# Small products of the scan and the attention in longer runs, both weight parts of the time steps in one operand, row sums of the modulation put off: a two-layer diffusion block on one core

## The chip, the core and the metric

The program runs on one core of one Trainium2 chip. The metric is the device time of one execution in microseconds (us), lower is better; the time before is the median of three runs. TensorE is PE in the profile, VectorE DVE, ScalarE ACT, GpSimd POOL; SP starts the transfers.

## The reference

Two layers over 256 context and 256 latent tokens of width 1024, everything in float32. Cut to what the change touches:

```
for layer in range(2):
    mod_l = split(silu(c) @ ada_w[layer] + ada_b[layer], 6)       # modulation, latent
    mod_c = split(silu(c_ctx) @ ada_w[layer] + ada_b[layer], 6)   # modulation, context
    h = modulate(rms_norm(tokens), shift, scale)
    # three branches on the same h, each gated, summed, projected
    #  scan (16 heads x 64, 2 groups, state 128, chunks of 128, forward and backward):
    dt = softplus(h @ w_dt + dt_bias); cs = cumsum(dt * a) in a chunk
    scores = einsum('bclgn,bcsgn->bcgls', cm, bm)
    y_diag = einsum('bcgls,bcgels,bcsgep->bclgep', scores, exp(cs_l - cs_s), x * dt)
    states = einsum('bcsgn,bcsge,bcsgep->bcgepn', bm, exp(cs_end - cs), x * dt)
    y_off  = einsum('bclgn,bcgepn,bclge->bclgep', cm, h_in, exp(cs))
    #  attention (8 heads x 64): context queries see 256 context keys; latent queries see
    #  a window of the latent grid plus all context keys (512 keys with a bias and mask)
    p = softmax(q @ k.T * 64 ** -0.5 + bias); o = p @ v
    #  conformer: gated linear unit, depthwise convolution of 31, layer norm, silu
    tokens += gate * (merged @ w_o)
    # then a gated feed-forward: dense in layer 0, top 2 of 8 experts in layer 1
```

Layer 1 computes latent tokens alone behind its keys, values and scan states.

## The kernel before

**Main products.** Every weight product runs as three products of two reduced-precision parts ("hi" and "lo", type fp32r): hi*hi, hi*lo, lo*hi. `wstat` (lines 205 to 207) keeps the weight as the stationary operand and streams 512 or 256 tokens; `wmov` (lines 251 to 253) streams the weight. `split` (lines 116 and 117) makes the parts: ACT copies to hi, DVE subtracts to lo. Small products (scores, transposes, scan) run in plain float32, two passes each but for the transposes.

**Order.** Each layer goes through a list of steps; for layer 0 `glu dt qkv xbc ssd g1 p1 g2 p2 z g0 p0`, where `xbc`, `z` and `g`/`p` (gate and branch projection) are main products and `ssd`, and behind qkv the attention, start generators. After each group of main products `pump` lets every running generator go on by its rate. A generator yields a number, its price in those units. So attention, scan, conformer and modulation are strewn between main products, and the compiler's scheduler fixes the order of each engine from priorities.

**Late issue.** `behind()` orders what is issued in it after the last main product on PE. `defer(queue, f, depth=2)` puts a piece of work in a queue and issues the oldest one so, once more than `depth` wait. `undefer` empties the queue.

**Banks and buffers.** Small results share four PSUM banks (`pw`), main sums have the other four (`acc`). A `pw` bank comes free when its reader (an ACT or DVE instruction) has read it; the next small product that gets it waits for that on PE, and the main products behind it wait too.

**Attention** (`attention`; scores L750 for latent, L770 for context queries). A head pair has heads j = 0, 1, whose 64-wide products lie in the two halves of the array's rows (64\*128 in the profile). Latent: for each of two query blocks, scores of both heads, bias add and maxima on DVE (L754 to L757), exp on ACT (L758, L759), then per head and block one deferred piece that transposes P on PE (L740) and copies it out (L742), and last `values` (L786, 128\*64: the array's columns halved). Scaling of P is L733.

**Scan** (`ssd`; the y part ends in L1094). For a chunk, a group of 8 heads and a direction r, in two halves of 4 heads (`hq`): M = exp of decays by ACT (L1054, L1055), times scores by DVE (L1056), and deferred the product of M with x\*dt (tile ydS, L1063, 128\*64, 4 heads). Then for each direction with a carried state E = exp(cs) (L1077), yoS (L1080) and adds on DVE. States: stS (L954), one per direction.

**Time steps** (`dt_path`, L865 to L867): 32 columns, eight blocks of k, three products each.

**Modulation** (`ada_v`): DVE accumulates weight rows times silu(c) (tile adac, L374) as the weights arrive over two buffers; a 32-column product (L382, 128\*32) sums over the partitions, for two column blocks j and the streams s; DVE adds it to the bias (L385). It runs as a generator, for layer 0 during z, g0 and p0, for layer 1 during the dense feed-forward.

Of the kernel before, what the change touches and what calls it, by code (L numbers as in the profile page):

```python
# [53 lines left out]
class Body:  # L54
# [298 lines left out]
    def ada_v(self, l, g):  # L353
# [6 lines left out]
        for j0 in (0, 2):  # L360
            accs = []
            for j in (j0, j0 + 1):
# [3 lines left out]
                for k in range(KD):  # L366
# [8 lines left out]
                    yield 0.7 * len(streams)  # L375
                    if j == 1 and k == 0:
                        self.keep()

            ps = self.pw(f"ada{l}{g}{j0}")
            for s in streams:  # L380
                for j, acc in zip((j0, j0 + 1), accs):
                    nc.tensor.matmul(ps[32 * j:32 * j + 32], self.con("oc")[:, 1 - s:33 - s], acc[:, s * 512:(s + 1) * 512],  # L382
                                     start=(s == streams[0]), stop=(s == 1), skip_group_check=True)
# [333 lines left out]
    def attention(self, l, q, kT, v, nt, o_):  # L717
# [4 lines left out]
        q_ = []  # L722
        for q0, nk, lat in streams:
            nkb = nk // 128
            for hp in range(4):
# [5 lines left out]
                def turn(P, j, qb, PT=PT, nm=nm, nk=nk, nkb=nkb, st=st):  # L731

                    nc.vector.tensor_scalar(P, P, st[:, j, qb, 5:6], None, op0=ALU.mult)  # L733

                    def turned():
                        if not PT:
                            PT.update({i: self.t4(f"PT{nm}{i}").rearrange("p (k t) -> p k t", t=256) for i in range(2)})
                        pt = self.pw(f"PT{nm}{j}{qb}")
                        for kb in range(nkb):
                            nc.tensor.transpose(pt[:, kb * 128:(kb + 1) * 128], P[:, kb * 128:(kb + 1) * 128], self.con("id"))  # L740
                        ev = nc.scalar.copy if j else nc.vector.tensor_copy
                        ev(PT[j][:, :nkb, qb * 128:(qb + 1) * 128], pt[:, :nk].rearrange("p (k t) -> p k t", t=128))  # L742
                    self.defer(q_, turned)
                if lat:
                    for qb in range(2):
# [17 lines left out]
                        for j in range(2):  # L763
                            turn(P[j], j, qb)
                            yield 1.7
                else:
# [6 lines left out]
                    for j in range(2):  # L773
# [5 lines left out]
                        for qb in range(2):  # L779
                            turn(P[j][:, qb * 256:(qb + 1) * 256], j, qb)  # L780
                        yield 1.5
# [7 lines left out]
                self.defer(q_, values)  # L789
                yield 0.5  # L790
        yield from self.undefer(q_)

# [61 lines left out]
    def dt_path(self, l):  # L854
# [3 lines left out]
        wH = self.t2("wdtH" + nm, F32R)[:, :KD * 32].rearrange("p (k n) -> p k n", k=KD)  # L858
        wL = self.t2("wdtL" + nm, F32R)[:, :KD * 32].rearrange("p (k n) -> p k n", k=KD)
        with self.prio("w"):  # L860
            nc.sync.dma_start(w, self.a["w_dt"][l])
            self.split(w, wH, wL)
# [6 lines left out]
        nc.scalar.activation(dT[0:32, :], ps[0:32, :], AF.Copy)  # L869
        pt = self.pw("dtt" + nm)  # L870
        for b in range(NB):
            nc.tensor.transpose(pt[:, b * 32:(b + 1) * 32], dT[0:32, b * 128:(b + 1) * 128], self.con("id")[0:32, 0:32])
# [5 lines left out]
        nc.vector.tensor_tensor(b3(x), b3(pt[:, :n]), bc(self.col("dtb")), op=ALU.add)  # L878
# [50 lines left out]
    def ssd(self, l, nt):  # L929
# [9 lines left out]
        def states(b, dirs, use):  # L939
# [6 lines left out]
            for g in range(G):  # L946
                px = self.xs_t(b, g, "s" + nm)
                for r in dirs:
                    xe = self.t2(f"xe{nm}{b}{r}{g}")
                    nc.vector.tensor_tensor(hd(xe), hd(px), hb(we, b, r, g), op=ALU.mult)  # L950

                    def state(r=r, g=g, xe=xe):
                        ps = self.pw(f"st{nm}{b}{r}{g}")
                        nc.tensor.matmul(ps, Bp[:, g * 128:(g + 1) * 128], xe, start=True, stop=True)  # L954
                        use(r, g, ps)
                    self.defer(q_, state)
                    yield 1.8
# [58 lines left out]
    def ssd_y(self, nm, b, hin, q_):  # L1016
# [23 lines left out]
        for g in range(G):  # L1040
# [5 lines left out]
            st = {}  # L1046
            for r in range(2):
                load(*((1, g) if r == 0 else (0, g + 1)))
                pb = cb[r, g]
                for hq in range(2):  # L1050
                    h0 = g * 8 + hq * 4
                    M = self.t2(f"M{nm}{b}{g}{r}{hq}").rearrange("p (h l) -> p h l", h=4)
                    for i in range(4):
                        nc.scalar.activation(M[:, i, :], pb[:, hq * 4 + i, :], AF.Relu, bias=cs[:, b, r, h0 + i:h0 + i + 1], scale=-1.0)  # L1054
                    nc.scalar.activation(M, M, AF.Exp, scale=-1.0)  # L1055
                    nc.vector.tensor_tensor(M, M, scm[:, r, g, None, :].to_broadcast([128, 4, 128]), op=ALU.mult)  # L1056

                    def diag(r=r, hq=hq, M=M, g=g, xd=xd, st=st):
                        if "pd" not in st:
                            st["pd"] = self.pw(f"yd{nm}{b}{g}")  # L1060
                        for i in range(4):
                            hl = hq * 4 + i
                            nc.tensor.matmul(st["pd"][64 * (i % 2):64 * (i % 2) + 64, (hl // 2) * 128:(hl // 2 + 1) * 128],  # L1063
                                             xd[r][:, hl * 64:(hl + 1) * 64], M[:, i, :],
# [747 lines left out]
```

## Time and profile before

| quantity | value |
|---|---|
| median of 3 runs | 2364.38 us (2364.26 to 2365.93) |
| the profiled execution | 2367.87 us |
| its span in the profile | 2366.1 us |
| TensorE's mean granted clock | 0.978 |
| PE busy | 2226.4 us, 94% of the span |
| DVE busy | 1509.5 us, 64% |
| ACT busy | 1030.1 us, 44% |
| the chain that ended last | PE 71%, issue 11%, DVE 7%, DMA 6%, ACT 4% |

Durations below come from the profiled execution, 3.5 us longer than the median. The end of a matmul is modelled, and matmuls overlap: a row's duration is longer than the time to the next start, so the costs here are taken from start to start. The program's stages in the profile: modulation and norms to 55 us, mixer of layer 0 to some 690, dense feed-forward to 1090, mixer of layer 1 to 1545, experts to the end.

### The profile page before, as it was taken

To read this page: it belongs to the slowest core of one execution; us is meant where nothing else is said; L and a number is where in the kernel's file an instruction comes from. 1 tells how busy PE (TensorE), PEld (TensorE's weight loads), DVE (VectorE), ACT (ScalarE), POOL (GpSimd) and SP (SyncE) were. 2 spreads that over 40 slices of the span, in tenths; PEclk is the share of its full clock that TensorE was granted. 3 is DMA by queue.
4 is the path that set the end of the run, shared out by engine and by line. 5 is a ranking of instruction groups with operands and counts; after the bars stand their busy time and mean duration, and the time that the engine had idled before them with its cause. 6 is when DMAs were issued, how large, how long until landed. Compare 5 with 4: busy or idle time off the path is not lost.

```text
span 2366.1 us, 29723 instructions
## 1 busy us (share of the span) xinstructions
PE 2226.4 (94%) x11075; PEld 1632.5 (69%) x11075; DVE 1509.5 (64%) x2384; ACT 1030.1 (44%) x1658; POOL 17.4 (1%) x32
## 2 busy tenths in 40 slices
PE   7999999699999999999999889899999989999897
PEld 3776677477777777788877779766655656566564
DVE  3667999787667665536898765743433555565556
ACT  4334673643342222225347685443332345454453
POOL 0000000000000000000000000000000000000000
PEclk9999999899999999999999999999999999999998
DMA  7232253445445556423423344488888899999995
GB/s 269 95 117 72 76 172 127 116 156 169 147 143 160 173 175 199 147 98 102 147 89 104 107 146 161 139 324 330 341 320 320 330 365 375 357 385 347 348 370 206
DMA packets 123658, 492.51 MB, mean 208 GB/s; under 512 B 12784, under 2 KB 23792, under 8 KB 89712
## 3 DMA queue, kind: packets, MB, share of 16 engines
q1 hardware_dynamic: 122656, 487.89, 57.4%
q10 hardware_dynamic: 848, 2.62, 0.3%
q8 instruction: 89, 1.46, 0.2%
q14 instruction: 65, 0.53, 0.1%
HBM read 488.24 MB, written 2.23 MB: 207 GB/s over the span
## 4 chain that ended last, share of the span: by engine, by line
PE 71%; issue 11%; DVE 7%; DMA 6%; ACT 4%; POOL 0%; SPq 0%; POOLq 0%; DVEq 0%; ACTq 0%
PE er L1546 8%; PE nn L1428 7%; PE e L1546 4%; DMA adaw<-in_ada_w_dram 4%; PE ndn L1453 4%; PE edr L1546 3%; PE ed L1546 2%; PE wg L205 2%; PE wg L207 2%; PE wg L206 2%; DVE adac L374 2%; PE xbcL L205 1%; PE xbcL L206 1%; PE xbcL L207 1%; PE fu L206 1%
## 5 line engine op out<-in xcount | busy, mean ns | idle before, releaser
L374 DVE SCALAR_TENSOR_TENSOR adac<-adaw,sc,adac 128x512 f32<-128x512 f32 x224 | 160.1, 747 | 57.3 <-DMA adaw<-in_ada_w_dram 56.7
L117 DVE TENSOR_TENSOR l_er<-r_er,h_er 128x1024 fp32r<-128x1024 f32 x132 | 154.5, 1218 | 59.9 <-ACT h_er L116 59.5
L1428 PE MATMUL nn<-r_ngun,xn 128*64 128x512 f32 (+1 forms) x768 | 168.2, 561 | 0.0
L116 ACT ACTIVATE h_er<-r_er 128x1024 fp32r<-128x1024 f32 x132 | 133.0, 1053 | 42.2 <-DMA r_er<-in_moe_gu_dram 29.4
L205 PE MATMUL wg<-hHm,h_wg 128*128 128x512 f32 (+1 forms) x384 | 135.7, 355 | 1.8 <-ACT g L682 1.1
L206 PE MATMUL wg<-hLm,h_wg 128*128 128x512 f32 (+1 forms) x384 | 129.9, 339 | 0.0
L207 PE MATMUL wg<-hHm,l_wg 128*128 128x512 f32 (+1 forms) x384 | 128.8, 339 | 0.5 <-DVE l_wg L117 0.4
L1546 PE MATMUL er<-h_er,gHp 128*128 128x512 f32 (+1 forms) x288 | 110.5, 389 | 17.7 <-ACT h_er L116 17.7
L1428 PEld LDWEIGHTS nn<-r_ngun,xn 128*64 128x64 f32 x768 | 54.2, 137 | 91.9 <-issue 85.1
L1546 PE MATMUL er<-h_er,gLp 128*128 128x512 f32 (+1 forms) x288 | 108.1, 381 | 0.0
L117 DVE TENSOR_TENSOR l_e<-r_e,h_e 128x1024 fp32r<-128x1024 f32 x44 | 52.2, 1222 | 63.5 <-ACT h_e L116 62.6
L1453 PE MATMUL ndn<-r_ndn,hnn 128*64 128x512 f32 x352 | 87.4, 598 | 0.0
L572 DVE SCALAR_TENSOR_TENSOR ccv<-cu,cols,ccv 128x488 f32<-128x488 f32 (+14 forms) x120 | 84.5, 729 | 1.0
L1443 DVE TENSOR_TENSOR hnn<-npn,nsn 128x256 f32<-128x256 f32 (+1 forms) x24 | 9.6, 401 | 117.6 <-ACT nsn L1441 117.6
L1433 ACT ACTIVATE ntn<-nn 128x512 f32<-128x512 f32 (+1 forms) x24 | 13.5, 561 | 162.7 <-PE nn L1428 162.7
L1546 PE MATMUL er<-l_er,gHp 128*128 128x512 f32 (+1 forms) x288 | 84.3, 381 | 0.0
L205 PEld LDWEIGHTS wg<-hHm,h_wg 128*128 128x128 f32 x384 | 72.7, 189 | 14.5 <-issue 4.0
L1546 PEld LDWEIGHTS er<-h_er,gHp 128*128 128x128 f32 x288 | 54.8, 190 | 40.2 <-ACT h_er L116 29.0
L116 ACT ACTIVATE h_wg<-r_wg 128x1024 fp32r<-128x1024 f32 x48 | 50.6, 1058 | 71.8 <-PE wg L206 52.0
L117 DVE TENSOR_TENSOR l_edr<-r_edr,h_edr 128x1024 fp32r<-128x1024 f32 x66 | 77.0, 1217 | 4.4 <-ACT h_edr L116 4.1
L207 PEld LDWEIGHTS wg<-hHm,l_wg 128*128 128x128 f32 x384 | 72.2, 189 | 10.1 <-DVE l_wg L117 2.1
L206 PEld LDWEIGHTS wg<-hLm,h_wg 128*128 128x128 f32 x384 | 72.8, 190 | 8.8 <-issue 2.3
(642 smaller groups left out, 5955.5 us busy)
## 6 DMA issues: line engine op xcount, KB each, us to landing
r_ngun<-in_moe_gu_dram SPq DMA_DIRECT2D x88, 1024.0 KB, 7.1
r_er<-in_moe_gu_dram SPq DMA_DIRECT2D x66, 1024.0 KB, 7.3
r_ndn<-in_moe_down_dram SPq DMA_DIRECT2D x44, 1024.0 KB, 7.6
adaw<-in_ada_w_dram SPq DMA_DIRECT2D x160, 256.0 KB, 3.1
r_edr<-in_moe_down_dram SPq DMA_DIRECT2D x33, 1024.0 KB, 7.4
r_wg<-in_w_in_dram SPq DMA_DIRECT2D x48, 512.0 KB, 3.6
r_e<-in_moe_gu_dram SPq DMA_DIRECT2D x22, 1024.0 KB, 7.6
cbS<-csd SPq DMA_DIRECT2D x24, 512.0 KB, 4.9
```

Source lines behind the costliest of these rows:

```text
L116: nc.scalar.activation(Hd, src, AF.Copy)
L117: nc.vector.tensor_tensor(Ld, src, Hd.bitcast(F32), op=ALU.subtract)
L205: mm(out, wh, xh, start=(first and kk == 0), stop=False, skip_group_check=True)
L206: mm(out, wh, xl, start=False, stop=False, skip_group_check=True)
L207: self.last = mm(out, wl, xh, start=False, stop=(kk == kc - 1), skip_group_check=True).ins
L374: nc.vector.scalar_tensor_tensor(d, w, c, d, op0=ALU.mult, op1=ALU.add)
L572: nc.vector.scalar_tensor_tensor(y[:, :, a:b], x[:, :, a + s:b + s], w[:, k:k + 1], y[:, :, a:b], op0=ALU.mult, op1=ALU.add)
L1428: mm(ps[64 * h:64 * h + 64, :n], x[kk], w[:, h, k, :], start=(kk == 0), stop=(kk == KD - 1), skip_group_check=True)
L1433: nc.scalar.activation(t, ps[:, :n], AF.Copy)
L1443: nc.vector.tensor_tensor(d, v[:, :, 1], g, op=ALU.mult)
L1453: mm(ps[64 * h:64 * h + 64], hT[:, kk * 64:(kk + 1) * 64], w[:, h, k, :], start=(kk == 0), stop=(kk == fc - 1), skip_group_check=True)
L1546: mm(ps[s][j], st[kk], w[p][:, k, :], start=(kk == 0 and p == 0 and q == 0), stop=(kk == kc - 1 and p == 1), skip_group_check=True)
```

## The change

- Row sums of the modulation (`ada_v`): one more yield before them, and all of a group issued in one `behind()`; the accumulation steps yield 0.64 for 0.7.
- Attention: a piece of transposes now covers both heads (and, for context queries, both query blocks; the copy out is twice as wide and half as many); depth 1 for 2. `values` is put in a list `joined` and issued by the next piece of transposes, ahead of them. Scores of a latent query block come with the price 3.4 in one yield.
- Time steps: hi and lo parts lie side by side as 64 columns, streamed once with the tokens' hi part; the tokens' lo part meets the 32 hi columns. The two halves of the sum are added on DVE behind the transposes.
- Scan: the products of both halves `hq` and of the directions' yoS in one deferred piece per direction; states of both directions in one piece; depth 1; E's loads are issued with the last M. The order of the adds changes, not their number.

```
-            ps = self.pw(f"ada{l}{g}{j0}")
-            for s in streams:
-                for j, acc in zip((j0, j0 + 1), accs):
-                    nc.tensor.matmul(ps[32 * j:32 * j + 32], ...
+            yield len(streams)
+            ps = self.pw(f"ada{l}{g}{j0}")
+            with self.behind():
+                for s in streams:
+                    for j, acc in zip((j0, j0 + 1), accs):
+                        nc.tensor.matmul(ps[32 * j:32 * j + 32], ...
...
+                    def turned():
...
+                        pts = [self.pw(f"PT{nm}{j}{qbs[0]}") for j in range(2)]
+                        n = len(qbs) * 128
+                        for f in joined:
+                            f()
+                        joined.clear()
+                        for j in range(2):
+                            for kb in range(nkb):
+                                for i, qb in enumerate(qbs):
+                                    c = kb * n + i * 128
+                                    nc.tensor.transpose(pts[j][:, c:c + 128], P[j][qb][:, kb * 128:(kb + 1) * 128], self.con("id"))
...
+                    self.defer(q_, turned, 1)
...
-                        for j in range(2):
-                            turn(P[j], j, qb)
-                            yield 1.7
+                        turn([{qb: p} for p in P], (qb,))
+                        yield 3.4
...
-                self.defer(q_, values)
-                yield 0.5
+                self.defer(q_, lambda f=values: joined.append(f), 1)
...
         for k in range(KD):
-            nc.tensor.matmul(ps[0:32, :], wH[:, k, :], self.h[0][k], start=(k == 0), stop=False)
-            nc.tensor.matmul(ps[0:32, :], wH[:, k, :], self.h[1][k], start=False, stop=False)
-            nc.tensor.matmul(ps[0:32, :], wL[:, k, :], self.h[0][k], start=False, stop=(k == KD - 1))
+            nc.tensor.matmul(ps[0:64, :], wp[:, k, :], self.h[0][k], start=(k == 0), stop=False, skip_group_check=True)
+            nc.tensor.matmul(ps[0:32, :], wp[:, k, 0:32], self.h[1][k], start=False, stop=(k == KD - 1), skip_group_check=True)
...
+                def diag(r=r, M=M, g=g, xd=xd, st=st, E=E):
...
+                    for hl in range(8):
+                        nc.tensor.matmul(st["pd"][...], xd[r][:, hl * 64:(hl + 1) * 64], M[r, hl // 4][:, hl % 4, :], ...
...
+                self.defer(q_, diag, 1)
+                yield 1.8 if r == 0 else 4.2
```

**PE in `xbc` of layer 0, scores of latent queries.** xbcL is the main product, PT are transposes, S scores (two in a row are heads 0 and 1 of one query block), po the values of an earlier head pair; what an instruction waits for stands behind it. Before:

```order
L750 MATMUL S_1641<-kTL_0_702,qL_0_700 128x512 [waits Activation_49]
L740 MATMUL PT_1632<-con_t,P_1566 128x128
L750 MATMUL S_1642<-kTL_0_702,qL_0_700 128x512 [waits PE_49]
L740 MATMUL PT_1632<-con_t,P_1566 128x128
L740 MATMUL PT_1662<-con_t,P_1567 128x128 [waits Activation_49]
...
L205 MATMUL xbcL_3_1518<-hHm_257,h_xbcL_3_1746 128x512
L206 MATMUL xbcL_3_1518<-hLm_259,h_xbcL_3_1746 128x512
L786 MATMUL po_1689<-PT_1583,vL_0_704 64x256 [waits DVE_49]
```

In the changed kernel:

```order
L751 MATMUL PT_1588<-con_t,P_1522 128x128 [waits DVE_49,PE_49,Activation_49]
...
L762 MATMUL S_1602<-kTL_0_694,qL_0_692 128x512
L762 MATMUL S_1603<-kTL_0_694,qL_0_692 128x512
L762 MATMUL S_1660<-kTL_0_694,qL_0_692 128x512 [waits Activation_49]
L762 MATMUL S_1661<-kTL_0_694,qL_0_692 128x512 [waits DVE_49]
L207 MATMUL xbcL_3_1495<-hHm_257,l_xbcL_3_1730 128x512
L797 MATMUL po_1686<-PT_1539,vL_0_696 64x256 [waits Activation_49]
```

The scores of two query blocks now stand together (four heads in a run, no transposes between), and the values, which need a fifth `pw` bank, come one main product behind them and wait for an ACT reader.

**PE in `g1` of layer 0, the scan's products.** wg is the main product, ydS the product of M with x\*dt, xtyS transposes, yoS the carried state's part. Before:

```order
L206 MATMUL wg_3_2433<-hLm_258,h_wg_0_2436 128x512
L1063 MATMUL ydS_2482<-MS_2419,xdS_2413 64x128 x4
L926 MATMUL xtyS_2569<-con_t,uL_4_1139 128x128 x2
...
L207 MATMUL wg_0_2430<-hHm_256,l_wg_1_2497 128x512
L1063 MATMUL ydS_2482<-MS_2454,xdS_2413 64x128 x4
L205 MATMUL wg_1_2431<-hHm_256,h_wg_1_2496 128x512
```

In the changed kernel:

```order
L207 MATMUL wg_0_2402<-hHm_256,l_wg_1_2468 128x512
L1094 MATMUL ydS_2488<-MS_2395,xdS_2389 64x128 x4
L1094 MATMUL ydS_2488<-MS_2426,xdS_2389 64x128 x4
L942 MATMUL xtyS_2537<-con_t,uL_4_1131 128x128 x2
L942 MATMUL xtyS_2537<-con_t,uL_6_1132 128x128 x2
L205 MATMUL wg_1_2403<-hHm_256,h_wg_1_2467 128x512
```

Two runs of four heads with ten main products between them have become one run of eight.

**PE in the dense feed-forward, row sums of the modulation.** fg, fu and fd are the main products, ada the row sums. Before:

```order
L207 MATMUL fg_2_5939<-hHf_5370,l_fg_2_6016 128x512
L382 MATMUL ada_6447<-adac_6031,con_t 32x512
L205 MATMUL fg_3_5940<-hHf_5370,h_fg_2_6015 128x512
...
L382 MATMUL ada_6447<-adac_6238,con_t 32x512
L382 MATMUL ada_6447<-adac_6031,con_t 32x512
L205 MATMUL fu_3_6103<-hHf_5370,h_fu_2_6182 128x512
...
L382 MATMUL ada_6447<-adac_6238,con_t 32x512
```

In the changed kernel:

```order
L253 MATMUL fd_1_6402<-h_fd_0_6407,f0L_0_5486 128x512
L384 MATMUL ada_6423<-adac_6007,con_t 32x512
L384 MATMUL ada_6423<-adac_6190,con_t 32x512
L384 MATMUL ada_6423<-adac_6007,con_t 32x512
L384 MATMUL ada_6423<-adac_6190,con_t 32x512
L251 MATMUL fd_2_6403<-h_fd_0_6407,f0H_0_5485 128x512
```

The four sums of a group, strewn over three places some 100 main products apart, stand in one run, some 100 main products later than the last of them stood.

## Rows read from the trace of the kernel before

**Rows 1.** Page, part 1: busy us (share of the span) and instructions of each engine

```profile
PE 2226.4 (94%) x11075; PEld 1632.5 (69%) x11075; DVE 1509.5 (64%) x2384; ACT 1030.1 (44%) x1658; POOL 17.4 (1%) x32
```

**Rows 2.** Busy time by windows: length; PE, PEld, DVE, ACT, POOL busy (instructions); PEclk; DMA

```profile
200.00:260.00 60.00, 59.89 (x265) 40.37 (x264) 55.64 (x119) 35.28 (x69) 0.00 (x0) 1.00 0.24 82
320.00:380.00 60.00, 60.00 (x338) 45.35 (x335) 55.97 (x91) 39.73 (x88) 0.00 (x0) 1.00 0.66 208
380.00:430.00 50.00, 49.92 (x259) 39.77 (x258) 43.94 (x65) 15.50 (x22) 1.05 (x1) 1.00 0.23 74
```

**Rows 3.** Waits of PE, 430 to 470 us: line and releaser: us, times, longest

```profile
PE wb0conf_out L205 <- ACT g L682: 11.4, 1, 11.4
PE ydS L1063 <- DVE MS L1056: 8.9, 3, 3.9
```

**Rows 4.** Timeline of PE, 341 to 343: start us, us, line, op, tiles, array shape, count

```profile
341.54 0.40 PE L207 MATMUL wg<-hHm,l_wg 128*128 128x512 f32 x1
341.87 0.66 PE L1063 MATMUL ydS<-MS,xdS 128*64 128x128 f32 x8
342.45 0.50 PE L205 MATMUL wg<-hHm,h_wg 128*128 128x512 f32 x1
```

**Rows 5.** Timeline of PE, 488 to 491: eight heads in a run

```profile
488.98 1.09 PE L1063 MATMUL ydS<-MS,xdS 128*64 128x128 f32 x16
```

**Rows 6.** Timeline of PE, 205 to 212: single scores, values in two pieces

```profile
207.65 1.12 PE L750 MATMUL S<-kTL,qL 64*128 64x512 f32 x2
208.70 0.44 PE L740 MATMUL PT<-con_t,P 128*128 128x128 f32 x2
209.07 0.65 PE L786 MATMUL po<-PT,vL 128*64 128x256 f32 x2
209.65 0.51 PE L207 MATMUL xbcL<-hHm,l_xbcL 128*128 128x512 f32 x1
210.08 1.08 PE L786 MATMUL po<-PT,vL 128*64 128x256 f32 x6
211.09 1.12 PE L750 MATMUL S<-kTL,qL 64*128 64x512 f32 x2
```

**Rows 7.** Timeline of PE, 277 to 280: two heads together

```profile
277.93 1.13 PE L750 MATMUL S<-kTL,qL 64*128 64x512 f32 x4
```

**Rows 8.** Timeline of PE, 1172 to 1175: four heads in a run

```profile
1172.48 1.99 PE L750 MATMUL S<-kTL,qL 64*128 64x512 f32 x8
```

**Rows 9.** Timeline of PE, 171 to 174: context scores between transposes

```profile
171.31 0.70 PE L770 MATMUL S<-kTL,qL 64*128 64x256 f32 x2
171.94 0.33 PE L740 MATMUL PT<-con_t,P 128*128 128x128 f32 x1
172.20 1.13 PE L770 MATMUL S<-kTL,qL 64*128 64x256 f32 x6
```

**Rows 10.** Timeline of PE, 89 to 91: time steps beside main products

```profile
90.06 0.39 PE L865 MATMUL dt<-hHm,wdtH 128*32 128x512 f32 x1
90.29 0.40 PE L866 MATMUL dt<-hLm,wdtH 128*32 128x512 f32 x1
```

**Rows 11.** Timeline of PE, 231 to 233: scores of a latent query block, first head

```profile
231.80 1.12 PE L750 MATMUL S<-kTL,qL 64*128 64x512 f32 x2
```

**Rows 12.** Timeline of ACT, 205 to 240: exp of latent scores

```profile
218.62 0.47 ACT L758 ACTIVATE P<-S,st 128x256 f32<-128x256 f32 x1
...
236.44 0.46 ACT L758 ACTIVATE P<-S,st 128x256 f32<-128x256 f32 x1
```

**Rows 13.** Timeline of PE, row sums: a whole group at 573, one in pieces from 777

```profile
573.88 1.91 PE L382 MATMUL ada<-adac,con_t 128*32 128x512 f32 x8
...
777.04 1.05 PE L382 MATMUL ada<-adac,con_t 128*32 128x512 f32 x2 [1.67 <-DVE adac L374]
...
800.85 1.05 PE L382 MATMUL ada<-adac,con_t 128*32 128x512 f32 x4 [0.76 <-DVE adac L374]
```

**Rows 14.** Waits of PE, 730 to 1090 us: the row sums

```profile
PE ada L382 <- DVE adac L374: 7.0, 9, 1.7
```

More of the change, by code (lines that the diff above doesn't have):

```diff
@@ L778, in attention @@
                         nc.vector.reciprocal(st[:, j, :, 5], st[:, j, :, 5])
-                        for qb in range(2):
-                            turn(P[j][:, qb * 256:(qb + 1) * 256], j, qb)
-                        yield 1.5
+                        yield 1.2
+                    turn([{qb: p[:, qb * 256:(qb + 1) * 256] for qb in range(2)} for p in P], (0, 1))
+                    yield 0.6
                 def values(hp=hp, PT=PT, nm=nm, nkb=nkb, q0=q0):
@@ L788, in values @@
                     self.split(po[:, 0:256], o_[0][hp][:, q0:q0 + 256], o_[1][hp][:, q0:q0 + 256])
-                self.defer(q_, values)
-                yield 0.5
+                self.defer(q_, lambda f=values: joined.append(f), 1)
         yield from self.undefer(q_)
+        yield 1.0
+        with self.behind():
+            for f in joined:
+                f()
     def conv31(self, cu, cv, nt):
@@ L947, in states, with state @@
                 px = self.xs_t(b, g, "s" + nm)
+                xe = {}
                 for r in dirs:
[L949 to L957, printed above, removed]
+                    xe[r] = self.t2(f"xe{nm}{b}{r}{g}")
+                    nc.vector.tensor_tensor(hd(xe[r]), hd(px), hb(we, b, r, g), op=ALU.mult)
+                def state(g=g, xe=xe):
+                    ps = {r: self.pw(f"st{nm}{b}{r}{g}") for r in dirs}
+                    for r in dirs:
+                        nc.tensor.matmul(ps[r], Bp[:, g * 128:(g + 1) * 128], xe[r], start=True, stop=True)
+                    for r in dirs:
+                        use(r, g, ps[r])
+                self.defer(q_, state, 1)
+                yield 1.8 * len(dirs)
         def step(dst, prev, b, r, g, ps):
@@ L1089, in fin @@
-            def fin(g=g, st=st):
-                prev = st["prev"]
-                nc.vector.tensor_tensor(prev, prev, st["pd"], op=ALU.add)
-                for i in range(4):
-                    y = u[g * 4 + i][:, bs]
-                    nc.vector.scalar_tensor_tensor(y, y, self.col("dsk", g * 4 + i), prev[:, i * 128:(i + 1) * 128], op0=ALU.mult, op1=ALU.add)
-            self.defer(q_, fin)
-            yield 1.2
+                        nc.scalar.activation(m[:, i, :], pb[:, hq * 4 + i, :], AF.Relu, bias=cs[:, b, r, h0 + i:h0 + i + 1], scale=-1.0)
@@ new lines, in ssd_y @@
+                    nc.scalar.activation(m, m, AF.Exp, scale=-1.0)
+                    nc.vector.tensor_tensor(m, m, scm[:, r, g, None, :].to_broadcast([128, 4, 128]), op=ALU.mult)
+                    if hq == 0:
+                        yield 1.8
+                E = {}
+                for d in range(2) if r else ():
+                    if hin[d] is None:
+                        continue
+                    E[d] = self.t2(f"E{nm}{b}{g}{d}").rearrange("p (i l) -> p i l", i=4)
+                    for j in range(2):
+                        nc.sync.dma_start(E[d][64 * j:64 * j + 64], rows(d, g).rearrange("(i j) l -> j i l", j=2)[j][None].to_broadcast([64, 4, 128]))
```

90 lines of the change are left out of this document (41 added, 49 removed).

## The prediction

> **What bounds the kernel now.** I read the engine shares of the profile's page first: TensorE is busy 94% of the span, VectorE 64%, ScalarE 44% [rows 1]. So the question is what PE's time is made of where the small products stand, and what would take over if they shrank. The windows come next: between 200 and 430 us, where attention and scan run beside `xbc` and the gates of layer 0, PE is busy without a gap, but DVE is close behind: 55.64 of 60 us, 55.97 of 60 and 43.94 of 50 [rows 2], together 155.55 of 170, so 14.45 us free. The waits of PE then show the one long stall of layer 0, between 430 and 470 us: 8.9 us for M and 11.4 us for a sigmoid [rows 3]; that work comes from ACT, which does the same instructions after the change. What is left are short timelines, from which each price is read as the distance between starts.
>
> **The price of an excursion.** A main product follows the last after some 0.23 us [rows 10]. A run of the scan's products starts 0.33 us behind the main product ahead of it, so entering costs 0.10; a run of four heads takes 0.58 us to the next main product [rows 4]. Eight heads in one run last 1.09 against 0.66 [rows 4, 5], 0.43 more. One join saves 0.58 - 0.43 + 0.10 = **0.25 us**. For scores: one head alone takes 1.05 us to the next start [rows 6], its row 1.12 long, two heads together 1.13 and four 1.99 [rows 7, 8]. So heads 0 and 1 in a run cost what one costs, and what stands between them (two transposes, a main product) makes them cost double.
>
> **Part by part**, with runs counted in the two orders:
>
> - *Scan products.* 29 runs become 16 in layer 0 and 13 become 12 in layer 1: 14 x 0.25 = **-3.5**. Transposes, yoS and states move too, but stand in the full array among main products; I cost them at nothing, bounded by 0.1 for each of some 20 places that are joined or split, either way.
> - *Latent scores.* Layer 0 has 12 lone heads and 2 pairs, afterwards 4 lone heads and 3 runs of four. With 1.05 for a lone head or a pair and 1.92 for four (1.99 less the 0.07 by which a row outlasts its run): 14 x 1.05 = 14.7 against 4.2 + 5.8 = 10.0, -4.7, and 7 fewer entries, -0.7. Layer 1 has 4 lone, 4 pairs and a run of four; afterwards 1 lone, 4 pairs, a run of three (2 x 1.05) and one of four: -1.1. Together **-6.5**.
> - *Context scores.* Three of four head pairs put one product between transposes, 0.63 us by itself while the remaining three take a whole run's time [rows 9]: 3 x (0.63 + 0.10) = **-2.2**.
> - *Transposes.* One between two scores takes 0.26 us [rows 9] where in a run of two the start-to-start is 0.37 for both, 0.18 or less each [rows 6]; 30 runs become 16 in layer 0, 14 become 10 in layer 1: 18 x some 0.1 = **-1.8**. The copies out of the context pairs halve in number on both engines; nothing waits for them in the full windows, so no gain is booked.
> - *Values.* A split-off product costs its own 0.58 us, since the other three still take 1.01 [rows 6]. Five pairs are split in layer 0, one afterwards; layer 1 has none split, and two cuts afterwards: 4 x 0.58 - 2 x 0.58 + entries = **-1.4**.
> - *Time steps.* 48 products of 512 columns become 32; at 0.23 each [rows 10] 16 x 0.23 = **-3.7**. They follow each other there without a wait, so only PE counts. DVE does one more add per layer, beside main products. Whether 64- and 32-column products in turn cost anything isn't in the trace; the 32-column ones stand beside full ones at the plain pace [rows 10], so I take 0. The upper bound is 0.1 for each of 32 products, +3.2.
>
>   The Trainium skill (TensorEngine Tiling (Array Packing), section Key Properties) says that a change of the tiling mode drains the engine. The 0.10 us at a scan run agrees with it; rows 10 don't, for by it these time steps should already have paid. By the skill's rule, priced with the row's 0.10 us, the 32 alternations would cost 3.2 us and the part would come to -0.5.
>
> - *Row sums.* A whole group takes 1.91 us [rows 13], in three pieces 3 x (0.98 + 0.10) = 3.2: 1.3 a group. The last group of layer 0 and the two of the first set in the feed-forward get joined (-1.3, -1.1, -1.3), the second and third of layer 0 are torn into three (+2.6). The first of layer 0 stands within the 11.4 us stall now [rows 3] and behind it afterwards, with 18 main products ahead of it: its 1.9 us are no longer covered. Waits for DVE in the feed-forward are 7.0 us [rows 14]; of those, the joined groups own 0.3 + 1.67 + 0.76 [rows 13], and put off by two units they find their sums done: -2.7. The other 4.3 us belong to later sets with one stream, whose weights come by DMA over two buffers; their row sums stay single and the last of each group still follows its last weight, so I leave them, with 4 either way in the range. Sum: **-1.9**.
> - *New waits.* Four latent scores fill all four `pw` banks. In six places of the order (four in layer 0, two in layer 1) values or the next scores then stand 0 to 11 main products behind. A bank comes free when exp has read it. The score that starts at 231.80 is read at 236.44 and done with at 236.90: 5.1 us [rows 11, 12]; one at 207.65 is read at 218.62, because DVE made the maxima late [rows 6, 12], 11.4 us. The four scores themselves cover 1.9 us, the main products behind them 0.2 to 2.5. That leaves between 0.7 and 9.3 us a place; in the nearest state (rows 11: scores in turn with transposes, DVE as full) 5.1 - 1.9 - 0.2 = 3.0 at three places, 0.7 at one, about 1 at two: 11.7. PE's pause lets DVE catch up, so part of it would have been lost to DVE anyway; I don't add that again. Moreover depth 1 brings the exps earlier in DVE's queue than the strewn pieces did; I take **+8**, ends 3 and 35.
>
> Loads of E are the same 40 broadcasts on SP, issued with the last M instead of after it; SP has nothing late there, and the exp that needs them now comes later. M of both halves stays in its buffer one piece longer; the nine buffers of that kind hold it exactly, so no cost, with the 8.9 us of rows 3 as the place where one would show.
>
> **Sum:** -3.5 - 6.5 - 2.2 - 1.8 - 1.4 - 3.7 - 1.9 + 8 = -13.0. The profiled execution took 2367.87 us (span 2366.1), 3.5 over the median; from the median 2364.4 the forecast is **2351.4 us**. What is shortened ahead of the 430 us stall does arrive: the scan reaches its last pieces by main products issued, so the ACT chain moves forward with PE.
>
> **Rivals.**
> 1. *DVE takes over.* In 200 to 430 us DVE has 14.45 us free over three windows [rows 2], but not where it is needed. If it is the bound there, every saving between 200 and 430 (scan -2.8, latent scores of layer 0 -5.4, half of transposes and values -1.5) turns into waits of PE for P and M. Left is -21.0 + 9.7 = -11.3, and +8 of bank waits: -3.3, about 2361 us, no change that can be told. For it: DVE at 93%. Against it: PE never once waited there before.
> 2. *Slower: banks held by scores.* Six places at the 207.65 us score's latency instead of the other's: 11.4 - 1.9 - 0.5 = 9 us each if DVE is behind everywhere, and the next transposes, main products and DVE work follow in a row, so the pauses don't overlap. At 5 us each, 30 us against 21 saved: +9, 2373 us. It decides from (21.0 + 4.7) / 6 = 4.3 us a place. For it: DVE's latency [rows 6, 12]. Against: once PE stops, nothing new is put on DVE, and 5.1 us are seen where DVE is as full.
> 3. *Putting off changes nothing.* If the row sums are bound by DMA all through, the 2.7 us come back and one more group falls into pieces: 2351.4 + 2.7 + 1.3 = 2355 us.
> 4. *Mode changes of the time steps.* By the alternation's upper bound the sum is 3.2 us worse: 2354.6 us. The skill's rule of above is its only support.
>
> **How the numbers follow.** The measurement can tell about 0.2%, 4.7 us, from no change. Forecast with rivals 3 and 4, which stay on its side: 0.70 (0.52, 0.10 and 0.08). DVE takes over: 0.16. Slower: 0.14. The forecast's own range is 2340 to 2360: 3 instead of 8 for the waits, 4 less in the row sums, 2 elsewhere, or the same upward. To leave out 2 in 10 at most it must take in rival 1 and the near part of rival 2: **2338 to 2368**. Faster 0.70, same 0.16, slower 0.14.
>
> **What would show it.** Right: ydS groups of 16, scores of eight instructions (four heads), 16 fewer products of the time steps, about 10 us less PE busy before 690 us, and new waits of PE for ACT's exp at L797 between 200 and 290 us of 2 to 4 us each. Rival 1: waits of PE at L751 or L1094 for DVE between 200 and 430. Rival 2: waits at L797 or L762 of over 4 us. Rival 3: row sums in the feed-forward wait as long as before, 7 us. Rival 4: time steps at over 0.3 us from start to start. The prediction is wrong if the sum of PE's waits in the two mixers grows by more than 15 us, or PE's busy time doesn't fall.

## The result and the profile after

| | before | changed |
|---|---|---|
| median of 4 runs each | 2364.32 us (2361.87 to 2365.93) | 2337.49 us (2334.51 to 2339.45) |
| ratio, 95% interval | 1 | 0.9886 (0.9869 to 0.9903) |
| the profiled execution | 2367.87 us | 2334.51 us |

The change saves 26.8 us, 1.1%, a little over twice the 13.0 us of the forecast and just outside its range (2338 to 2368). The direction was right and rival 2 (slower) did not come about; the size was wrong.

The page's part 1 of the changed kernel, beside [rows 1]:

```profile
PE 2196.9 (94%) x11059; PEld 1622.7 (70%) x11059; DVE 1509.3 (65%) x2382; ACT 1034.8 (44%) x1657; POOL 17.4 (1%) x32
```

PE's busy time fell by 29.5 us, DVE's didn't move, ACT's rose by 4.7, and PE is as full as before. To see where, both traces are cut at the first main product of each stage (starts read from the timelines, lengths in us; the last four columns are the experiments with one part of the change alone, below):

```
stage                                before  changed | steps  rows  attention  scan
start, glu dt qkv of layer 0, from     29.4     28.3 |
  length                              135.8    131.4 | 132.1  133.8   134.4   134.0
xbc g1 p1 g2 of layer 0               299.6    287.9 | 298.4  299.8   291.2   297.2
p2 z g0 p0 and w_o of layer 0         240.5    238.3 | 240.8  246.7   238.6   235.9
dense feed-forward                    398.7    392.8 | 399.2  397.6   399.8   399.2
glu dt qkv of layer 1                  95.5     93.9 |  92.4   94.0    94.0    94.0
xbc g1 p1 of layer 1                  161.3    164.8 | 162.8  158.7   165.4   164.1
g2 z p2 g0 p0 of layer 1              139.3    132.6 | 138.8  138.0   139.3   131.5
w_o of layer 1 and experts            866.1    862.6 | 865.1  865.0   865.8   863.3
```

The two profiled executions are 33.4 us apart, more than the medians: some 7 us lie in the start, ahead of the first changed instruction, and in the experts, which the change doesn't touch. The rest is a fall of 11.7 in layer 0's middle, 2.2 behind it, 5.9 in the feed-forward, 3.7 by the time steps, 6.7 at the end of layer 1's scan, and a rise of 3.5 in layer 1's xbc to p1. A stage's length also moves with the granted clock, whatever the edit: p2 of layer 1, with 0.2 us of waiting each time, took 17.5 us at a clock of 1.00 (time steps alone) and 20.0 at 0.86 (the changed kernel), and xbc to p1 of layer 1 took 158.7 and 162.8 us in two experiments that leave it as it was. So 2 or 3 us in one stage of one execution show little.

The timeline of PE where scores of two query blocks now stand together (answers [rows 6 to 8]):

```profile
220.50 1.03 PE L751 MATMUL PT<-con_t,P 128*128 128x128 f32 x8
221.46 1.99 PE L762 MATMUL S<-kTL,qL 64*128 64x512 f32 x8
223.38 0.49 PE L207 MATMUL xbcL<-hHm,l_xbcL 128*128 128x512 f32 x1
224.87 1.95 PE L797 MATMUL po<-PT,vL 128*64 128x256 f32 x16 [0.99 <-ACT P L770]
```

and what ACT did meanwhile (answers [rows 12]):

```profile
224.25 0.47 ACT L770 ACTIVATE P<-S,st 128x256 f32<-128x256 f32 x1 [2.10 <-DVE st L769]
```

Four heads take 1.92 us to the next start, as forecast. The values do wait for the exp that frees a bank, but 0.99 us and not 3: the exp of the first head starts 2.8 us behind the scores here, 4.6 us in [rows 11, 12]. At the other two places it starts 5.1 and 2.8 us behind them, with eleven and two main products in between for one here. PE's waits from 160 to 360 us:

```profile
PE po L797 <- ACT P L770: 2.7, 3, 1.0
PE wg L205 <- ACT h_wg L116: 1.0, 1, 1.0
```

Three places, 2.7 us, and no wait on DVE at all, although DVE is fuller than before (answer [rows 2]):

```profile
200.00:260.00 60.00, 58.04 (x293) 43.36 (x293) 58.12 (x131) 42.41 (x86) 0.00 (x0) 1.00 0.27 93
320.00:380.00 60.00, 60.00 (x353) 48.06 (x350) 58.67 (x93) 37.34 (x72) 0.00 (x0) 1.00 0.60 183
```

The long stall of layer 0 (answer [rows 3], 160 to 450 us) is what it was, 20.7 us for 20.3:

```profile
PE wb0conf_out L205 <- ACT g L684: 12.9, 1, 12.9
PE ydS L1094 <- DVE MS L1075: 7.8, 4, 3.3
```

The time steps (answer [rows 10]) start 0.23 us apart, 64 columns or 32:

```profile
86.37 0.39 PE L880 MATMUL dt<-hHm,wdtp 128*64 128x512 f32 x1
86.60 0.39 PE L881 MATMUL dt<-hLm,wdtp 128*32 128x512 f32 x1
86.83 0.39 PE L880 MATMUL dt<-hHm,wdtp 128*64 128x512 f32 x1
```

Row sums in the feed-forward, first the joined groups from the timeline (answer [rows 13]), then PE's waits from 686 to 1078 us (answer [rows 14]):

```profile
747.32 1.91 PE L384 MATMUL ada<-adac,con_t 128*32 128x512 f32 x8
...
805.61 1.91 PE L384 MATMUL ada<-adac,con_t 128*32 128x512 f32 x8
```

```profile
PE ada L384 <- DVE adac L374: 4.2, 2, 3.1
```

The joined groups wait for nothing; what is left are two waits, of 1.1 and 3.1 us, in the later sets, where six waits had 4.3 us before.

The end of layer 1's scan is where the forecast saw nothing. The ACT table loads there by line, before (1378 to 1414 us: sigmoid L682, exp of M, exp of E):

```profile
L682 ACT ACT_TABLE_LOAD x7 | 9.0, 1283 | 0.1
L1055 ACT ACT_TABLE_LOAD x3 | 3.8, 1283 | 0.1
L1077 ACT ACT_TABLE_LOAD x3 | 3.8, 1283 | 0.1
```

and in the changed kernel (1353 to 1384 us):

```profile
L684 ACT ACT_TABLE_LOAD x5 | 6.4, 1283 | 0.1
L1074 ACT ACT_TABLE_LOAD x3 | 3.8, 1283 | 0.1
L1092 ACT ACT_TABLE_LOAD x2 | 2.6, 1283 | 0.0
```

Thirteen became ten, on the engine that was the fullest there (ACT 35.2 us busy of 36 before, PE 29.5). In the whole kernel the loads rose from 63 to 66: what counts is where they stand. The windows over g2 and z of layer 1, before and changed:

```profile
1360.70:1434.40 73.70, 66.22 (x535) 60.55 (x534) 45.39 (x71) 60.37 (x102) 0.00 (x0) 0.95 0.50 157
```

```profile
1337.60:1403.00 65.40, 60.94 (x518) 56.93 (x517) 42.57 (x67) 53.36 (x90) 0.00 (x0) 1.00 0.53 163
```

73.7 us became 65.4, ACT's busy time fell by 7.0, and PE's mean clock rose from 0.95 to 1.00. Three loads are 3.8 of those 7.0. Nearly all the rest is work on M that now stands ahead of g2, by ACT's groups in the two windows, before:

```profile
L1054 ACT ACTIVATE MS<-cbS,cs 128x128 f32<-128x128 f32 x39 | 12.7, 388 | 0.0
L1055 ACT ACTIVATE MS<-MS 128x512 f32<-128x512 f32 x10 | 6.1, 622 | 0.1
```

and changed:

```profile
L1073 ACT ACTIVATE MS<-cbS,cs 128x128 f32<-128x128 f32 x32 | 10.1, 389 | 0.0
L1074 ACT ACTIVATE MS<-MS 128x512 f32<-128x512 f32 x8 | 5.0, 623 | 0.1
```

PE too has 17 products fewer in the window (535 and 518); they stand in the stage ahead of it.

### The profile page after: what moved, and what is told of

Its sections match the earlier page's. It is cut to its first block, busy times and chain, and to the rows that moved or that the text cites. A ratio compares the mean times of both kernels' runs of the same rounds, so it can differ in the third digit from the quotient of the medians.

```text
span 2332.7 us, 29682 instructions
## 1 busy us (share of the span) xinstructions
PE 2196.9 (94%) x11059; PEld 1622.7 (70%) x11059; DVE 1509.3 (65%) x2382; ACT 1034.8 (44%) x1657; POOL 17.4 (1%) x32
## 4 chain that ended last, share of the span: by engine, by line
PE 69%; issue 10%; DVE 10%; DMA 5%; ACT 4%; POOL 0%; SPq 0%; POOLq 0%; DVEq 0%; ACTq 0%
PE er L1563 8%; PE nn L1445 7%; PE e L1563 4%; PE ndn L1470 4%; PE edr L1563 4%; DMA adaw<-in_ada_w_dram 3%; PE ed L1563 2%; DVE ccv L574 2%; PE wg L205 2%; PE wg L207 2%; PE wg L206 2%; PE xbcL L205 1%; PE fu L206 1%; PE xbcL L206 1%; PE fu L205 1%
## 5 line engine op out<-in xcount | busy, mean ns | idle before, releaser
L574 DVE SCALAR_TENSOR_TENSOR ccv<-cu,cols,ccv 128x482 f32<-128x482 f32 (+14 forms) x120 | 85.3, 730 | 1.1
L1563 PE MATMUL er<-l_er,gHp 128*128 128x512 f32 (+1 forms) x288 | 84.5, 382 | 0.0
L207 PEld LDWEIGHTS wg<-hHm,l_wg 128*128 128x128 f32 x384 | 72.2, 190 | 11.7 <-issue 2.2
```

The source lines that it names most:

```text
L207: self.last = mm(out, wl, xh, start=False, stop=(kk == kc - 1), skip_group_check=True).ins
L574: nc.vector.scalar_tensor_tensor(y[:, :, a:b], x[:, :, a + s:b + s], w[:, k:k + 1], y[:, :, a:b], op0=ALU.mult, op1=ALU.add)
L1563: mm(ps[s][j], st[kk], w[p][:, k, :], start=(kk == 0 and p == 0 and q == 0), stop=(kk == kc - 1 and p == 1), skip_group_check=True)
```

## The experiments

Theory A: each part is worth the PE time that its own joined runs save, and the parts add up. Its rivals differ by part and stand with the runs. Times are medians, each against runs of the kernel before on the same chip; the two kernels with a copy for the sigmoid have one time each. In the code, lines are left out at `...`, and of each part alone only telling lines of its hunk stand.

**One part of the change at a time** (four runs). Each edit is that part's hunk of the diff ahead, applied to the kernel before: `dt_path`; `ada_v`; `attention`; the two of `ssd`.

```
e_dt    +            nc.tensor.matmul(ps[0:64, :], wp[:, k, :], ...
e_ada   +            yield len(streams)
        +            with self.behind():
e_att   +                    self.defer(q_, turned, 1)
        +                self.defer(q_, lambda f=values: joined.append(f), 1)
e_scan  +                self.defer(q_, state, 1)
        +                self.defer(q_, diag, 1)
```

*Time steps.* 

> The kernel before with the time steps' part alone (hi and lo weight parts side by side). Theory A (each part is worth the PE time that its own shorter or joined runs save, and the parts add up): 16 fewer 512-column products at 0.23 us, -3.7 us, PE's time on the tile dt 11.0 to 7.4 us. Rival (64 and 32 columns in turn cost a switch each): -0.5 us and products over 0.3 us from start to start; the run of the whole change already speaks against it. If later stages answer to the shift (waits that come or go), the time differs from -3.7 by more than 2 us.

*Row sums.* 

> The kernel before with the row sums' part alone (one more yield, one behind for the group, price 0.64). Theory A: feed-forward stage 398.7 to about 393 us (idle -4, joins -2), first groups of layer 0 as in the whole change (+2.9 us of row-sum time behind the stall, -3.1 inside it), so -4 to -6 us in all. Rival B (the sums are bound by the weights' arrival, and the gain in the feed-forward came from the other parts' shift): idle of the feed-forward stays at 12 to 13 us, total -2 us or less.

*Attention.* 

> The kernel before with the attention's part alone. Theory A: xbc to g2 of layer 0 about -10 us (scores -6.7, values -2.7, transposes -1.3, entries -2 to -3, new waits of PE for exp at the values +2.7), layer 1's xbc to p1 +3 us, the rest unchanged: -6 to -8 us. Rival C (the gain of layer 0's middle needs the scan's part too, since DVE is full there): -3 us or less, with waits of PE between 200 and 430 us.

*Scan.* 

> The kernel before with the scan's part alone (states and y products in longer runs). Theory A: 14 joins of 0.25 us, -3.5 us, ydS and entries only. Rival D (the scan's part is worth most by the waits that it takes away at the end of layer 1's scan: fewer ACT table loads between exp and sigmoid, since two E and two M come one behind the other): the stages g2, z, p2 of layer 1 fall by 5 to 8 us, table loads of layer 1's scan fall by 3 or more, total -8 to -12 us.

| alone | median | before beside it | ratio (95%) |
|---|---|---|---|
| time steps | 2361.08 | 2362.33 | 0.9996 (0.9985 to 1.0008) |
| row sums | 2359.75 | 2362.33 | 0.9988 (0.9977 to 0.9999) |
| attention | 2358.56 | 2362.33 | 0.9988 (0.9977 to 0.9999) |
| scan | 2349.82 | 2362.33 | 0.9949 (0.9935 to 0.9964) |

The time steps took their 3.7 us off PE (the products of dt 11.0 to 7.4 us), which the whole time can't resolve.

The row sums alone gave the feed-forward 1.1 us and cost layer 0's second half 6.2. The first number doesn't decide between A and B: PE's idle time there fell by 2.0 us, from 13.2 to 11.2, but the clock of this execution was 0.99 for 1.00, and PE's busy time rose by 1.0 although the sums' own time fell.

The attention won 8.4 us in layer 0's middle, with no wait on DVE added between 200 and 360 us, and lost 4.1 in layer 1, where ACT's table loads from xbc to p1 rose from 15 to 22 and PE's idle time by 3.3 us. Its time, 3.8 us less, lies between the two expectations; rival C falls by its sign, the waits on DVE, that did not come.

The scan gave 12.5 us where its 14 joins are worth 3.5. By the stages layer 0 fell by 7.0 (PE's idle time by 3.4 of them), the stages from g2 to p0 of layer 1 fell by 7.8, and those ahead of them rose by 2.8. Rival D is right about the place and the three loads (29 became 26 in layer 1's scan), but more than half of the gain lies elsewhere; what the loads are worth is the question of the next pair.

The parts don't add up. The four medians differ from the kernel before by 1.3, 2.6, 3.8 and 12.5 us, 20.1 in all, where the whole change saves 26.8.

**Is it ACT?** The gates of layer 1's third branch are copied and not passed through the sigmoid, with and without the scan's part:

```
-                   lambda o, ps: self.nc.scalar.activation(g[o], ps, AF.Sigmoid)
+                   lambda o, ps: self.nc.scalar.activation(g[o], ps, AF.Copy if (l, br) == (1, 2) else AF.Sigmoid)
```

> The kernel before; the gates of the third branch in layer 1 are copied and not passed through the sigmoid (so that part of the output's computation is left out), which takes every ACT table load for them out of the scan's end. Theory T (the 7.7 us that the change saves in z of layer 1 were ACT's: 13 table loads between 1378 and 1414 us, 10 after): g2, z and p2 of layer 1, 92.5 us before, fall by 8 us or more, and PE's clock stays at 1.00 there. Rival P (they were PE's: joins and an earlier end of the scan): they fall by 3 us or less.

> The same copy for the sigmoid, in the kernel with the scan's part alone. Theory T: against the kernel before with the same copy, g2, z and p2 of layer 1 differ by 2 us or less (the joins alone), for there are no table loads left to save. Rival P: they are 6 us or more shorter, as with the sigmoid (7.7 us in z).

Each has one time only (2354.69 and 2343.01 us), so the stages decide: g2, z and p2 of layer 1 took 92.5 us before, 81.6 with the copy; 84.5 with the scan's part, 78.9 with both. So the copy alone takes 10.9 us away, and behind it the scan's part is worth 2.7 instead of 8.0. Some 5.3 of those 8 us hang on ACT, as Theory T has it. The 2.7 that are left are more than T's 2, and no joins: layer 1 has one run less. They match the 15 products fewer that PE has in the window with the scan's part (534 and 519), 2.6 us of its busy time. The windows over g2 and z, of the kernel before with the copy and of the scan's part with it:

```profile
1357.50:1420.30 62.80, 61.72 (x534) 58.09 (x533) 45.13 (x71) 42.91 (x89) 0.00 (x0) 1.00 0.60 184
```

```profile
1353.00:1413.00 60.00, 59.14 (x519) 56.66 (x518) 42.51 (x68) 40.33 (x80) 0.00 (x0) 1.00 0.57 177
```

PE has 1.1 and 0.9 us left to wait, at a clock of 1.00, where the kernel before had 7.5 us at 0.95. That ACT bound this place is shown by this. That it was the three loads is not: the copy takes out all thirteen, and ACT was relieved as much by the work on M that moved ahead (3.7 us) as by three loads (3.8 us). No run has the one without the other.

The Trainium skill (ScalarE: Activation LUTs, section What ACT_TABLE_LOAD costs) gives a load 1283 ns and a drain of about 1380 ns more. The rows agree on the first and not on the second: the timeline of ACT before shows an activation ending, the load, and the next one in step:

```profile
1386.98 0.63 ACT L1077 ACTIVATE ES<-ES 128x512 f32<-128x512 f32 x1
1387.63 1.28 ACT L682 ACT_TABLE_LOAD   x1
1388.92 0.38 ACT L682 ACTIVATE g<-wg 128x256 f32<-128x256 f32 x1
```

By the rows three loads fewer are 3.8 us of ACT. By the Trainium skill's figures, three switches fewer would be 8.0 us, an estimate.

**The row sums taken back from the whole.**

```
-                    yield 0.64 * len(streams)
+                    yield 0.7 * len(streams)
...
-            yield len(streams)
             ps = self.pw(f"ada{l}{g}{j0}")
-            with self.behind():
...
```

> The changed kernel with the row sums' part taken back. Theory A (the part saves PE waits and joins in the feed-forward whatever else is changed): feed-forward from 392.8 to about 398 us, second half of layer 0's mixer about 3 us shorter (sums inside the stall again, none torn): time +1 to +3 us against the whole change. Rival B (alone the part gave the feed-forward only 1.1 us and cost layer 0 some 6; the 5.8 us in the whole come from where its groups fall): layer 0 gets 3 to 6 us shorter, feed-forward 4 to 6 us longer, net zero within 1.5 us.

2346.32 against 2363.60 us, ratio 0.9932 (0.9907 to 0.9957), so 9.5 us behind the whole change; by the stages 5.2 (feed-forward 398.7 us for 392.8, layer 0's g2 93.1 for 90.7). That is more than either expectation. The feed-forward did what theory A said, the torn groups in layer 0 gave nothing back. In company the part is worth 9.5 us, alone 2.6: the 6.9 between them are about what the sum of the four parts alone lacks. Why its time exceeds its stages isn't settled; the runs of this kernel spread over 13 us.

**Attention of before in layer 1** (`attention1` is the attention of the kernel before).

```
-            jobs[1] = self.spawn(self.attention(l, q, kT, v, nt, r[1]), ...
+            jobs[1] = self.spawn((self.attention1 if l else self.attention)(l, q, kT, v, nt, r[1]), ...
...
```

> The changed kernel with the attention of before in layer 1 (its new form in layer 0 alone). Theory A (the attention's part gives back in layer 1, through waits and slower transposes and values, about half of what it saves in layer 0): stages xbc, g1, p1 of layer 1 fall from 164.8 to about 161 us, time -3 to -4 us against the whole change. Rival (the loss there is the scan's, whose part alone showed +2.8 us in those stages): no gain, within 1.5 us.

2336.59 us, ratio 0.9889 (0.9866 to 0.9912): no difference from the whole change that the time can tell; the three stages fell from 164.8 to 163.1 us. That decides little, for the same stages took 158.7 to 162.8 us where no edit touches them. PE's idle time in them, 8.8 us before, was 12.1 with the attention alone, 10.9 in the whole and 10.0 here; with the scan alone (164.1 us) it was 8.7, and with the scan and the copy the stages took 161.1. So part of the loss is the attention's; that the scan has a part in it is not shown.

**Values not joined.**

```
-                self.defer(q_, lambda f=values: joined.append(f), 1)
+                self.defer(q_, values, 1)
```

> The changed kernel with the values of the attention deferred as a piece of their own, depth 1, and not joined to the next piece of transposes. The waits of PE at L797 for exp (0.99, 0.97 and 0.76 us between 224 and 263 us) are then put elsewhere. Theory A (the bank wait costs about 1 us a place, not 3, so the join pays for it): no gain, +0 to +3 us by more entries. Rival (the bank-holding run is the dear part, its cost hidden in DVE's and ACT's lateness behind it): xbc and g1 of layer 0 fall by 3 us or more.

2344.03 us, ratio 0.9930 (0.9911 to 0.9949), 7.7 us slower than the whole, where theory A had 0 to 3. The wait for exp is gone (0.4 us at L797, for another reason), but values and scores now cut each other, from the timeline of PE:

```profile
219.82 0.65 PE L797 MATMUL po<-PT,vL 128*64 128x256 f32 x2
220.39 1.12 PE L762 MATMUL S<-kTL,qL 64*128 64x512 f32 x2
221.45 0.65 PE L797 MATMUL po<-PT,vL 128*64 128x256 f32 x4
222.16 1.12 PE L762 MATMUL S<-kTL,qL 64*128 64x512 f32 x2
```

Start to start, scores and values of layer 0's middle take 6.1 us more, and xbc to g2 of layer 0 takes 5.6. A bank wait of 2.7 us in all buys that; the rival falls.

**Put off further, and one table for ACT: three more versions.** The gate of layer 1's third branch as 1 / (1 + exp(-x)), the sums put off by 3 units (layer 0) and 4 (layer 1), and both with the attention of before in layer 1:

```
-            yield len(streams)
+            yield 3.0 + l
...
-                   lambda o, ps: self.nc.scalar.activation(g[o], ps, AF.Sigmoid)
+                   lambda o, ps: self.sig(g[o], ps, (l, br) == (1, 2)), ...
...
+        nc.scalar.activation(g, ps, AF.Exp, scale=-1.0)
+        nc.vector.tensor_scalar(g, g, 1.0, None, op0=ALU.add)
+        nc.vector.reciprocal(g, g)
```

> The changed kernel with the row sums put off further: 3 units in layer 0's set, 4 in the feed-forward, instead of 1 or 2. By the order all 8 groups then stand in one run each. Theory A (a put-off long enough takes the waits away and joins the groups): layer 0's second half -2.6 us (two torn groups joined), feed-forward from 392.8 to about 385 us (4.2 us of waits at L384 gone, four pairs joined at 0.85 each), -8 to -10 us against the whole change. Rival (the sums are bound by the weights' arrival, and the wait moves with them): feed-forward falls by 2 us or less.

> The changed kernel with the third branch's gate in layer 1 as 1 / (1 + exp(-x)): exp on ACT, add and reciprocal on DVE, so ACT keeps one table through the scan's end. Theory T: g2, z and p2 of layer 1 fall from 85.5 to about 80 us (the copy instead of the sigmoid gave 5.6 us with the scan's part), -4 to -6 us against the whole change. Rival (DVE, with 8 x 2 more instructions, now ends last there): -1 us or slower.

> The changed kernel with both of these and the attention of before in layer 1. If the three are independent: -8 to -10 by the put-off, -4 to -6 by the gate, -1 to -3 by the attention, so -13 to -18 us against the whole change, about 2321 us. If they eat the same waits: -8 to -12 us.

| | median | before beside it | ratio (95%) |
|---|---|---|---|
| put off further | 2329.41 | 2363.08 | 0.9855 (0.9834 to 0.9875) |
| gate by exp | 2332.95 | 2363.08 | 0.9877 (0.9857 to 0.9897) |
| both, and layer 1's attention | 2323.77 | 2363.08 | 0.9842 (0.9823 to 0.9860) |

Put off further: the feed-forward takes 384.6 us (385 forecast), no wait of PE at L384 is left, and the later sets' sums stand in pairs, as in its timeline of PE:

```profile
856.34 1.05 PE L384 MATMUL ada<-adac,con_t 128*32 128x512 f32 x4
857.32 0.50 PE L205 MATMUL fu<-hHf,h_fu 128*128 128x512 f32 x1
```

So the sums were not bound by the weights' arrival, as the forecast had it of the later sets; they were issued too early. By the medians this version is 6.8 us ahead of the change, a little less than the 8 to 10 expected.

The gate by exp: g2 and z took 61.2 us for 65.4, with one table load for eleven in ACT's rows. DVE, 56.0 us busy of those 61.2, is not yet in the way. With p2, which had a higher clock here, the three stages took 80.1 us for 85.5. By the medians it is 3.3 us ahead, under the 4 to 6 expected.

Both together, with layer 1's attention of before, are 39.3 us under the kernel before and 12.5 under the change: between the two expectations. Of the three, only this one is clear of the change by its interval; those of the first two overlap with the change's (0.9869 to 0.9903).

## Why the prediction was wrong

- **Scan products, -3.5.** The step that failed: the term prices the scan's part by PE's joins alone, with transposes, yoS and states at nothing, and the sum has no term for PE's waits on ACT and DVE in g2 and z of layer 1, as if these stayed. The prediction looked at one long stall, layer 0's, and of that one its sentence that ACT "does the same instructions after the change" came out (20.3 and 20.7 us). The joins themselves are worth what was said: the runs fell from 42 to 28, and 17 of these are eight heads long, 1.02 us each at the full clock. But the part alone is worth 12.5 us. In g2 and z of layer 1, where ACT was the bound, its order changed: ten table loads for thirteen and less work on M, so that PE's idle time fell from 7.5 to 4.5 us and its clock rose to 1.00. The copy experiments show that some 5.3 of the 8 us there hang on ACT. This is the largest miss.
- **Latent and context scores, -8.7.** By the trace, scores went from 28.6 to 20.8 us in both mixers, start to start and without waits: -7.8, beside their entries. Right.
- **Transposes, -1.8; values, -1.4.** Together -3.2, measured +0.8 and -3.9: together right, apart not. Layer 1's transposes became dearer (7.0 to 9.1 us) by the clock: 16 of them behind a wait of 3.8 us on P took 3.69 us at a granted clock of 0.50, where 8 take 0.92 at the full one.
- **Time steps, -3.7.** Right to a tenth. Rival 4 falls: 64 and 32 columns in turn start 0.23 us apart. No run here shows a cost of a change between these two shapes, though the rule of the Trainium skill (TensorEngine Tiling (Array Packing), section Key Properties) would have it.
- **Row sums, -1.9.** Near, in part by luck. The joined groups' waits of 2.7 us went as forecast, and the torn groups and the uncovered one cost layer 0 2.9 us of sums (3.2 forecast). Of the 4.3 us of waits that were left in place 4.2 stayed, but as two waits for six, and the reason was wrong: the last sum of each group was not held by its last weight, for put off further all those waits went. The feed-forward fell by 5.9 us, where joins and waits there were forecast at 5.1. Rival 3 falls.
- **New waits, +8.** Mis-sized: 2.7 us at the values of layer 0 and 2.1 more idle time in layer 1's xbc to p1, 4.8, or 5.8 with the one for a weight. A place costs 1 us, not 3: at two of the three places exp starts 2.8 us behind the scores, and at the third, with 5.1, eleven main products cover it. That DVE makes the maxima sooner because the scores come together is likely and not tested. Rival 2, which took the longest latency for all places, falls by the same rows. Its price was also read from the wrong row: by the order of the heads the exp at 218.62 us reads the score that started at 201.16, and that of 207.65 is read at 220.53, 12.9 us later; it changes nothing here.
- **Rival 1.** It falls: PE waits on DVE nowhere between 160 and 418 us, although DVE is fuller than before (58.12 us of 60 from 200 to 260, 58.67 from 320 to 380). The waits for M behind that, 7.8 us, are the start of layer 0's stall, 8.9 before.
- **The sum.** From glu of layer 0 to layer 1's w_o, the two executions differ by 28.8 us. PE's busy time fell by 26.8 of them, where the terms for PE's own work say 18.3 (21.0 less the 2.7 of waits), and its idle time by 2.0, where the terms for waits say +5.3 (8 less 2.7). So the miss is about half in waits that went or never came and half in busy time; the clock behind the waits is some of the second half, and the rest of it isn't split up by these runs. The range was built on more waits alone; fewer were not among its bounds.

## What to carry to other kernels

Price the joins by start-to-start distances, they held here; but for every engine whose order the change moves, find the stages that it bounds before the change, count there its table loads and the work that moves in or out, and give the range an end for waits that vanish. Work that waits for slow accumulation is put off until the order shows its pieces side by side; a short bank wait can be cheaper than the cuts that avoid it.

## What the runs showed that was not expected

A wait can cost more than its length. In the changed kernel the 3.1 us wait for a row sum is followed by products at 0.43 us from start to start instead of 0.23:

```profile
915.35 1.81 PE L384 MATMUL ada<-adac,con_t 128*32 128x512 f32 x2 [3.08 <-DVE adac L374]
917.08 0.80 PE L206 MATMUL fu<-hLf,h_fu 128*128 128x512 f32 x1
917.67 0.63 PE L207 MATMUL fu<-hHf,l_fu 128*128 128x512 f32 x1
918.10 0.63 PE L205 MATMUL fu<-hHf,h_fu 128*128 128x512 f32 x1
```

The window from 915 to 922 us has a granted clock of 0.76, a mix of the full 2.4 GHz and 1.2, the next one 1.00 again:

```profile
915.00:922.00 7.00, 6.65 (x20) 4.14 (x21) 3.35 (x5) 1.06 (x1) 0.00 (x0) 0.76 0.38 123
922.00:930.00 8.00, 8.00 (x37) 6.64 (x36) 5.34 (x8) 2.85 (x4) 0.00 (x0) 1.00 0.70 232
```

The row sum itself took 1.73 us to the next start for 0.98, and the four products behind it 1.86 for some 1.03 elsewhere: 1.6 us more behind a wait of 3.1. A shorter wait for a sum, the 1.67 us of [rows 13], had no such tail: the clock is 1.00 from 775 to 785 us. The same lies in the end of layer 1's scan before the change, 0.75 from 1400 to 1410 us:

```profile
1400.00:1410.00 10.00, 7.19 (x47) 5.88 (x48) 6.59 (x12) 9.92 (x19) 0.00 (x0) 0.75 0.38 108
```

PE had stood for 2.8 us of those 10, in pieces, with ACT busy for 9.92. In the changed kernel a window of that stage with nearly as much standing, in pieces too, stays at 1.00:

```profile
1360.00:1370.00 10.00, 7.53 (x64) 6.51 (x63) 6.28 (x11) 9.84 (x17) 0.00 (x0) 1.00 0.21 67
```

So the idle time of a window alone doesn't tell whether the clock falls in it.
